# A two-layer decoder trunk: gates begun before the queries are done, one result slot, query groups moved in the order, and key weights with their own memory

## The chip, the cores and the metric

One core of one Trainium2 chip runs the whole program. The metric is the device time of one execution in microseconds (us), lower is better. TensorE (PE) multiplies matrices, VectorE (DVE) and ScalarE (ACT) do elementwise work, GpSimd (POOL) does powers and fills, SyncE (SP) issues the DMAs. PEld is PE's weight loader.

## What is computed

512 prompt tokens and 64 sample tokens (8 sequences of 8) pass through two layers. Cut to what matters:

```python
h = rmsnorm(x, g_norm)                                   # 1024 channels
rq, rk, rv, rz, aq, ak, av, az, iq, ik, iw, gr, ga = in_projection(h, w_in, ...)
o_r, s_new = retention(rq, rk, rv, ret_s0)               # 4 heads, state 128 x 128
u_r = (group_norm_heads(o_r) * silu(rz)) @ w_o_ret
# indexer: score = sum_h relu(iq_h . ik) * iw_h ; keep the top 128 (prompt) or 66 (sample) keys
o_a = softmax attention of aq over the kept keys          # 8 query heads, 2 key heads of 64
u_a = (o_a * silu(az)) @ w_o_att
m = sigmoid(gr) * u_r + sigmoid(ga) * u_a                 # the gates: 1024 channels each
x = x + m @ w_out
x = x + sigmoid(x @ w_ple_gate) * (p_i @ w_ple_proj)
```

Keys, values, indexer keys and retention states are outputs too.

## The kernel before

**Numbers and tiles.** All 576 tokens are handled together. A float32 product is made of three matmuls in a reduced-precision float32 form: each operand is split into a high part (`xh`, `whi`, by ACT) and a rest (`xl`, `wlo`, by DVE), and high x high, rest x high and high x rest are added up. Where channels are the rows of the result (`proj_a`: az, rq, rk, rz, gr, ga, wout, wpg), one unit gives 128 channels by 576 tokens in two halves of 288 columns, 24 matmuls each. Where tokens are the rows (`proj_b`: iq, rv, aq; `proj_kx`: the keys), a unit runs over five token tiles `j`, of which 0 to 3 are the prompt and 4 is the sample.

**The order.** The program is written as many generators ("streams"). A planner in the kernel (`Streams.go`, line 284) simulates the five engines with a table of durations (`_duration`) and emits next, of all streams' next instructions, the one that could start first; ties go to the smaller priority number. So it fixes each engine's order before anything runs. `Event` and `Slots` only steer the planner; on the chip the waits are semaphores. Priorities are in `PRIO`: 0 for the evacuations of projections and weight conversion, 3 for attention and the sample's indexer, 4 for sample retention, 5 for sample attention, 6 for prompt retention, 7 for the prompt's indexer with its top-k.

**The main stream** (priority 9) is the projections in the order of `PLAN`, one after another: kx, iq, rv0, rv1, az0 to az3, rt0, aq0, rt1, aq1, rt2, rt3 (rt is rq, rk and rz of a head), then the 16 gates gr and ga, then merge (wo), wout, pp, wpg. It writes into three PSUM banks "pm", and each half or tile is evacuated by a stream of its own.

**Weights** come by DMA into two staging tiles `WST` and are split into three pairs `WHI`, `WLO` by `convert`, which give their staging tile back. `drop` frees a pair after its unit.

**Side streams.** `indexer(j)` scores keys and finds the top-k on DVE. `attend` takes the query groups (j, u) in order: j = 0 to 3, u = 0, 1 (aq0 and aq1). Each is two `pair` streams that add into the one bank "oT", then `collect` multiplies the result, from POOL, into the tile `silz`. A query tile stays in one of four slots `QS` until its group is through. `attend_s` uses "oT" for the sample. `ret_p(h)` and `ret_s(h)` do the retention of head h, one head at a time; when both have used the head's rotated q and k, they set `e_hd[h]`. The buffers for q and k alternate between two heads, so `ropeT` of head 2 waits for `e_hd[0]` and of head 3 for `e_hd[1]`. The prompt state leaves through the small tiles `SO` and the store `out_rsp`.

**The gates** (line 1306) wait, before gr0, as follows, and then take one of four slots `ZS` in the tile `misc`, whose columns the query and indexer evacuations use before:

```python
if name == "gr" and i[0] == 0:
    for e in list(e_q.values()) + list(e_iq.values()) + [e_k, e_rr]:
        yield e
    ZS = zslots(0, 4)
z = yield Get(ZS)
```

A gate's two halves are multiplied with `R` (DVE, misc<-pm,R) and passed through tanh (ACT); `spill` then stores the gate to DRAM (`zgr`, `zga`), from where the merge fetches it. The merge starts when all side streams are done, by splitting `silz` into `oh` and `ol`.

**The start.** `load(k)` brings x by channel tile, and after x0 the norm gains `gn`, which the first split of x needs; `load_weights` brings the key weights in five parts (`KX_PARTS`) through `WST`. `setup2` brings the constants and the page table. `proj_kx` runs as x and weights arrive.

Of the kernel before, what the change touches and what calls it, by code (L numbers as in the profile page):

```python
# [11 lines left out]
FT = mybir.dt.float32  # L12
FR = mybir.dt.float32r
# [3 lines left out]
OP = mybir.AluOpType  # L17
# [88 lines left out]
class Op:  # L106
    __slots__ = ("eng", "fn", "a", "k", "name", "outs", "ins", "dur", "form", "banks")

    def __init__(self, eng, fn, name, a, k):
# [9 lines left out]
        if eng in ("DVE", "ACT") and len(self.ins) and self.outs[0][1] != self.ins[0][1]:  # L119
            self.dur += 0.12  # L120
# [25 lines left out]
def _duration(eng, name, out, aps, a, k):  # L146
# [21 lines left out]
    if eng == "POOL":  # L168
        return 0.3 + (0.165 if k.get("op", a[-1]) == OP.pow else 0.0022) * n
# [154 lines left out]
def tile_hybrid_decoder(ctx: ExitStack, tc: tile.TileContext, A, O):  # L324
# [51 lines left out]
    WST = slots(cp, "wst", [128, 1024], FT, 2)  # L376
    WHI = slots(cp, "whi", [128, 1024], FR, NSLOT["hi"])
    WLO = slots(cp, "wlo", [128, 1024], FR, NSLOT["lo"])
# [32 lines left out]
    second, third = Event(), Event()  # L411
# [4 lines left out]
    class Unit:  # L416
        def __init__(self, srcs):
            self.srcs, self.parts, self.ev = srcs, [], Event(len(srcs))
            self.evs = [Event() for _ in srcs]

    def plan(l):
# [7 lines left out]
        for st in PLAN:  # L429
# [3 lines left out]
            elif name == "iq":  # L433
                srcs = b(("wq",), 260, 3)
# [10 lines left out]
            u = Unit(srcs)  # L445
# [5 lines left out]
    def load_weights(units):  # L451
        for n, (u, src, size) in enumerate(units):
            if n == 1:
                yield second
            if n == 3:
                K.set(third)
            t = yield Get(WST)
            yield SP.dma_start(t[:, :size], src)
            K.spawn(convert(u, t, size, stage_ev[n], stage_ev[n + 1]), PRIO["convert"])

    def convert(u, t, size, prev, done):
        yield prev
        hi = yield Get(WHI)
        lo = yield Get(WLO)
        yield S.activation(hi[:, :size], t[:, :size], AF.Copy)
        yield V.tensor_tensor(lo[:, :size], t[:, :size], hi[:, :size].bitcast(FT), OP.subtract)
        K.put(WST, t)
# [52 lines left out]
    def proj_kx(u, xh, xl, evs):  # L520
# [3 lines left out]
        for i, (k0, k1) in enumerate(KX_PARTS):  # L524
# [16 lines left out]
            K.put(WHI, u.parts[i][0])  # L541
            K.put(WLO, u.parts[i][1])
# [17 lines left out]
    def put_x(x, k, l, xh, xl, zs, first):  # L560
        yield S.activation(xh[:, k, :T], x, AF.Copy, scale=gn[:, l, k:k + 1])
        yield V.scalar_tensor_tensor(xl[:, k, :], x, gn[:, l, k:k + 1], xh[:, k, :T].bitcast(FT),
                                     op0=OP.mult, op1=OP.subtract)
        yield S.activation(xh[:, k, T:TX], xl[:, k, NP:T].bitcast(FT), AF.Copy)
        if k == 0:
# [12 lines left out]
    def layer(l, xh, xl, kxb):  # L578
# [15 lines left out]
        e_r, e_rq, e_rr = Event(), Event(), Event()  # L594
# [45 lines left out]
        SO = slots(at, "so", [128, 128], FT, 2)  # L640
# [22 lines left out]
        def tables():  # L663
            yield e_rq
            yield SP.dma_start(rot, A["rot"])
            yield V.tensor_tensor(cosr, cosr, R, OP.mult)
# [170 lines left out]
        def indexer_s():  # L837
            yield paged
            kt = yield Get(S4)
            for b in range(8):  # L840
# [438 lines left out]
        la = None  # L1279
        for st in PLAN:  # L1280
# [4 lines left out]
            elif name == "iq":  # L1285
                yield from proj_b(U("iq"), 260, 3, xh, xl, (1, 4, 2, 3), iqx)
# [19 lines left out]
            elif name in ("gr", "ga"):  # L1306
                if name == "gr" and i[0] == 0:
                    for e in list(e_q.values()) + list(e_iq.values()) + [e_k, e_rr]:
                        yield e
                    ZS = zslots(0, 4)  # L1310
                z = yield Get(ZS)
                ev = Event(2)

                def gate(z, ev):
                    def evac(ps, cs):
                        yield V.tensor_tensor(z[:, cs], ps[:, :TH], R[:, cs], OP.mult)
                        K.put(BANK["pm"], ps)
                        yield S.activation(z[:, cs], z[:, cs], AF.Tanh, scale=0.5)
                        K.set(ev)
# [3 lines left out]
                def spill(z, ev, dst):  # L1323
                    yield ev
                    yield SP.dma_start(dst, z)
                    K.put(ZS, z)

                K.spawn(spill(z, ev, zd[(l,) + st]), 0)
                yield from proj_a(U(*st), 0, mv, KT, gate(z, ev))
# [68 lines left out]
        pst = lb.tile([128, 2, T], FT, name="pst")  # L1398

# [79 lines left out]
        def ple2(d, th, ev):  # L1479
# [3 lines left out]
            else:  # L1483
# [4 lines left out]
                yield from put_x(xa[:, d], d, l + 1, nh, nl, ZS, e_sq)  # L1488
                K.set(e_n[d])
                yield SP.dma_start(xd[:, d, :], xa[:, d])  # L1490
            K.set(e_e)
# [13 lines left out]
    def main():  # L1505
# [13 lines left out]
        def load(k):  # L1519
            x = st.tile([128, T], FT, name=f"x{k}")  # L1520
            if k > 3:
                yield third
            yield SP.dma_start(x, A["xT"][:, k, :])
            if k == 0:
                yield SP.dma_start(gn, A["norm_gain"])
                K.set(second)
            yield from put_x(x, k, 0, xh, xl, zs, e_sq)
            K.set(evs[k])

        for k in range(KT):  # L1530
            K.spawn(load(k), 2 if k else 0)
# [9 lines left out]

KX_PARTS = ((0, 1), (1, 2), (2, 4), (4, 6), (6, 8))
# [18 lines left out]
NSLOT = dict(s4=3, qs=4, t2=5, pt=1, hi=3, lo=3)  # L1561


def _prepare(x_prompt, x_sample, cache_k, cache_v, cache_idx_k, state_ret, page_table, p_prompt, p_sample,
# [13 lines left out]
    d["norm_gain"] = c(chan(norm_gain).transpose(2, 0, 1))  # L1578
    d["qk_gain"] = c(np.stack([np.asarray(q_norm_gain), np.asarray(k_norm_gain)], 1).reshape(-1))
    d["xT"] = c(chan(tok(x_prompt, x_sample)).transpose(2, 1, 0))  # L1580
# [63 lines left out]
```

## Time and profile before

| | us |
|---|---|
| median of 3 runs | 1098.57 |
| lowest, highest | 1097.22, 1099.5 |
| the profiled execution | 1100.1 |
| its span, first to last instruction | 1098.2 |
| PE busy | 1074.9 (98%) |
| DVE busy | 759.6 (69%) |
| ACT busy | 527.4 (48%) |

Busy PE is modelled, since matmuls are pipelined; the number of PE instructions in a stretch tells more than its busy time. Layer 0 runs from 0 to about 570 us and layer 1 from there to the end, with the same stages: keys, projections with attention and retention beside them (DVE nearly full), gates, merge, output projections. All instructions of the program are recorded at one line, so groups are told apart by the names of tiles: a matmul pm<-xh,whi is a `proj_a` unit, pm<-whi,xh a `proj_b` tile.

### The profile page before, as it was taken

What the parts mean: (1) busy time and instruction counts of PE and PEld (TensorE: products, weight loads), DVE (VectorE), ACT (ScalarE), POOL (GpSimd) and SP (SyncE); (2) the same over time, 40 slices, a digit from 0 to 9 for tenths busy, and PEclk for the clock granted to TensorE, in tenths of its full rate; (3) what the DMA queues carried; (4) which work ended last, traced back from release to release, by engine and by line L of the source; (5) the groups of instructions that cost most, each with busy time, mean ns of one, the idle gap of its engine ahead of it and who ended that gap; (6) DMA issues with size and microseconds to landing.
All of it is one profiled execution on the core that took longest, in us unless ns stands there. A gap on an engine that the chain in (4) does not pass through costs nothing.

```text
span 1098.2 us, 21521 instructions
## 1 busy us (share of the span) xinstructions
PE 1074.9 (98%) x8330; PEld 1048.6 (95%) x8330; DVE 759.6 (69%) x1963; ACT 527.4 (48%) x1112; POOL 68.6 (6%) x110
## 2 busy tenths in 40 slices
PE   7999999999999999999999999999999999999998
PEld 7989999989999999999999998999899999999998
DVE  6799999985455576543658999999854556655343
ACT  6743355676455442335446433656654555222421
POOL 0200012111000000000011001121101000000000
PEclk9999999999999999999999999999999999999999
DMA  6531222223333265533344322223232324554231
GB/s 204 162 118 69 88 80 96 76 83 110 113 103 108 103 198 158 184 93 104 99 124 133 108 71 74 81 99 106 91 121 91 121 90 144 184 184 136 82 115 49
DMA packets 53112, 124.85 MB, mean 114 GB/s; under 512 B 7443, under 2 KB 19603, under 8 KB 53011
## 3 DMA queue, kind: packets, MB, share of 16 engines
q1 hardware_dynamic: 53010, 123.49, 34.7%
q8 instruction: 65, 1.06, 0.4%
q14 instruction: 37, 0.30, 0.1%
HBM read 103.12 MB, written 20.35 MB: 112 GB/s over the span
## 4 chain that ended last, share of the span: by engine, by line
PE 68%; DVE 24%; issue 3%; DMA 1%; ACT 1%; SPq 1%; POOL 0%; DVEq 0%; POOLq 0%; ACTq 0%
PE pm L309 57%; DVE xl L309 6%; DVE sm L309 4%; DVE wlo L309 3%; PE tq L309 3%; PE oT L309 3%; DVE misc L309 2%; PE ta L309 2%; PE acc L309 2%; DVE silz L309 2%; PE tr L309 1%; DVE iqs L309 1%; DVE qs L309 1%; DVE tb L309 1%; DVE t2k L309 1%
## 5 line engine op out<-in xcount | busy, mean ns | idle before, releaser
L309 PE MATMUL pm<-xh,whi 128*128 128x288 f32 x1536 | 458.1, 298 | 0.0
L309 PE MATMUL pm<-xh,wlo 128*128 128x288 f32 x1536 | 457.5, 298 | 0.0
L309 PE MATMUL pm<-xl,whi 128*128 128x288 f32 x1536 | 457.2, 298 | 0.0
L309 PEld LDWEIGHTS pm<-xh,whi 128*128 128x128 f32 x1536 | 290.1, 189 | 1.2
L309 PEld LDWEIGHTS pm<-xl,whi 128*128 128x128 f32 x1536 | 290.2, 189 | 1.1 <-issue 0.2
L309 PEld LDWEIGHTS pm<-xh,wlo 128*128 128x128 f32 x1536 | 289.8, 189 | 0.9
L309 ACT ACTIVATE whi<-wst 128x1024 fp32r<-128x1024 f32 (+4 forms) x148 | 149.9, 1016 | 202.3 <-PE pm L309 135.0
L309 DVE TENSOR_TENSOR wlo<-wst,whi 128x1024 fp32r<-128x1024 f32 (+4 forms) x148 | 174.1, 1178 | 78.1 <-ACT whi L309 77.7
L309 PE MATMUL pm<-wlo,xh 128*128 128x256 f32 (+2 forms) x416 | 115.8, 287 | 1.7 <-DVE wlo L309 1.7
L309 PE MATMUL pm<-whi,xh 128*128 128x256 f32 (+2 forms) x416 | 117.0, 288 | 0.0
L309 PE MATMUL pm<-whi,xl 128*128 128x256 f32 (+2 forms) x320 | 91.6, 286 | 0.0
L309 ACT ACTIVATE t2k<-t2k,sm 128x256 f32<-128x256 f32 (+3 forms) x110 | 63.1, 579 | 43.7 <-DVE sm L309 42.2
L309 PEld LDWEIGHTS pm<-wlo,xh 128*128 128x128 f32 x416 | 78.7, 189 | 2.5 <-DVE wlo L309 2.3
L309 PEld LDWEIGHTS pm<-whi,xh 128*128 128x128 f32 x416 | 78.8, 189 | 1.9 <-issue 1.6
L309 PE MATMUL pm<-oh,whi 128*128 128x288 f32 x240 | 70.9, 296 | 0.0
L309 PE MATMUL pm<-oh,wlo 128*128 128x288 f32 x240 | 70.9, 295 | 0.0
L309 PE MATMUL pm<-ol,whi 128*128 128x288 f32 x240 | 70.8, 295 | 0.0
L309 PEld LDWEIGHTS pm<-whi,xl 128*128 128x128 f32 x320 | 60.5, 189 | 0.1
L309 DVE TENSOR_TENSOR misc<-pm,R 128x288 f32<-128x288 f32 x64 | 29.1, 455 | 42.1 <-PE pm L309 41.2
L309 DVE MAX8 sm<-xl 128x8 f32<-128x384 f32 (+2 forms) x96 | 52.2, 550 | 1.0
L309 DVE MATCH_REPLACE8 xl<-sm,xl 128x256 f32<-128x256 f32 (+2 forms) x96 | 51.7, 540 | 0.0
L309 DVE TENSOR_TENSOR ptl<-ta,pth 128x512 fp32r<-128x512 f32 (+1 forms) x48 | 28.6, 597 | 28.0 <-ACT pth L309 27.9
(261 smaller groups left out, 1723.7 us busy)
## 6 DMA issues: line engine op xcount, KB each, us to landing
wst<-in_wa SPq DMA_DIRECT2D x96, 512.0 KB, 3.5
wst<-in_wb SPq DMA_DIRECT2D x16, 512.0 KB, 4.0
wst<-in_wo SPq DMA_DIRECT2D x16, 512.0 KB, 3.9
zgr<-misc SPq DMA_DIRECT2D x16, 288.0 KB, 2.0
zga<-misc SPq DMA_DIRECT2D x16, 288.0 KB, 2.1
misc<-zgr SPq DMA_DIRECT2D x16, 288.0 KB, 2.8
misc<-zga SPq DMA_DIRECT2D x16, 288.0 KB, 4.6
s<-in_ckv SPq DMA_DIRECT2D x32, 128.0 KB, 2.4
```

Source lines behind the costliest of these rows:

```text
L309: op.fn(*op.a, **op.k)
```

## The change

- **Gates.** gr0 waits only for `e_k` (keys done) and `e_rq` (`R` done). There is one slot `ZS` at first; a stream `more` adds three when all queries and indexer tiles are done. The slot is now taken by the evacuation of a gate's first half, not ahead of its matmuls, and the second half's evacuation stores the gate itself.
- **Order.** aq0 goes ahead of az0, aq1 ahead of rt1.
- **Key weights.** The converted key weights of both layers have tiles of their own (`kxw`), and in layer 0 the raw ones too (`kxs`), so they take no `WST`, `WHI` or `WLO` (in layer 1 they still pass `WST`). In layer 0 their loads are issued at set places between those of x (`STEPS`), and the first conversion is on DVE.
- **Norm gains** come as 16 more columns of x0 (`x0`) and are copied to `gn` by POOL; the first split of x reads them from x0 itself. All x are issued by one stream, and the constants after them.
- **Buffers of 1040 columns** let iq's weights come in two parts of four channel tiles instead of three of up to three.
- **One `SO`** instead of two. The sample's gathers wait for the issue of the `rot` table. In the output stage the square of x comes after its split and its store.
- **The planner's table**: match_replace takes 60 columns more, a fill on POOL 0.32 us, an ACT instruction with up to 64 partitions 0.12 us more (instead of any with shifted partitions).

The diff, cut to its core:

```diff
-        if eng in ("DVE", "ACT") and len(self.ins) and self.outs[0][1] != self.ins[0][1]:
+        if eng == "DVE" and len(self.ins) and self.outs[0][1] != self.ins[0][1]:
+            self.dur += 0.12
+        if eng == "ACT" and self.outs[0][2] - self.outs[0][1] <= 64:
             self.dur += 0.12
...
+        if name == "match_replace":
+            return (n + 124) / 0.96e3
...
-    WST = slots(cp, "wst", [128, 1024], FT, 2)
+    WST = slots(cp, "wst", [128, 1040], FT, NSLOT["st"])
...
-                srcs = b(("wq",), 260, 3)
+                srcs = b(("wq",), 260, 4)
...
     def load_weights(units):
         for n, (u, src, size) in enumerate(units):
-            if n == 1:
-                yield second
-            if n == 3:
-                K.set(third)
-            t = yield Get(WST)
+            own = None
+            if u.kx is not None:
+                yield go_kx[n] if u.kx == 0 else e_kxw
+                a, z = (k * 320 for k in KX_PARTS[u.srcs.index((src, size))])
+                own = [w[:, a:z] for w in kxw[u.kx]]
+            if u.kx == 0:
+                t = kxw["raw"][:, a:z]
+            else:
+                t = yield Get(WST)
             yield SP.dma_start(t[:, :size], src)
...
+        if first:
+            yield V.tensor_copy(hi[:, :size], t[:, :size])
+        else:
+            yield S.activation(hi[:, :size], t[:, :size], AF.Copy)
...
-        SO = slots(at, "so", [128, 128], FT, 2)
+        SO = slots(at, "so", [128, 128], FT, 1)
...
             elif name in ("gr", "ga"):
-                if name == "gr" and i[0] == 0:
-                    for e in list(e_q.values()) + list(e_iq.values()) + [e_k, e_rr]:
-                        yield e
-                    ZS = zslots(0, 4)
-                z = yield Get(ZS)
-                ev = Event(2)
+                if ZS is None:
+                    yield e_k
+                    yield e_rq
+                    ZS = zslots(0, 1)
+
+                    def more():
+                        for e in list(e_q.values()) + list(e_iq.values()):
+                            yield e
+                        for z in zslots(1, 4).free:
+                            K.put(ZS, z)
+
+                    K.spawn(more(), 0)
...
+                        if cs.start == 0:
+                            z = yield Get(ZS)
...
+                        if cs.start:
+                            yield ev
+                            yield SP.dma_start(dst, z)
+                            K.put(ZS, z)
...
+        if l + 1 < DEPTH:
+            kxw[l + 1] = kx_tiles(lb, l + 1)
+            K.set(e_kxw)
...
+        def load():
+            for k in range(KT):
+                x = st.tile([128, T if k else T + DEPTH * KT], FT, name=f"x{k}")
+                yield SP.dma_start(x, A["xT"][:, k, :] if k else A["x0"])
+                K.spawn(take(k, x), 0)
+                if k in STEPS:
+                    K.set(go_kx[STEPS.index(k)])
+            K.set(third)
...
+STEPS = (0, 1, 3, 5, 7)
...
-PLAN = _plan("kx iq rv0 rv1 az0 az1 az2 az3 rt0 aq0 rt1 aq1 rt2 rt3")
+PLAN = _plan("kx iq rv0 rv1 aq0 az0 az1 az2 az3 rt0 aq1 rt1 rt2 rt3")
```

## Rows read from the trace of the kernel before

**Rows 1.** The page, busy time, share of the span and instructions of each engine.

```profile
PE 1074.9 (98%) x8330; PEld 1048.6 (95%) x8330; DVE 759.6 (69%) x1963; ACT 527.4 (48%) x1112; POOL 68.6 (6%) x110
```

**Rows 2.** Stretches: length, busy time (instructions) of each engine, clock, DMA share, GB/s.

```profile
120.00:238.00 118.00, 114.74 (x923) 110.76 (x922) 114.07 (x362) 66.10 (x157) 18.99 (x25) 1.00 0.26 87
238.00:250.00 12.00, 9.84 (x52) 8.07 (x51) 8.27 (x20) 7.59 (x20) 0.09 (x1) 0.72 0.24 87
250.00:262.00 12.00, 12.00 (x125) 11.04 (x124) 6.16 (x29) 6.53 (x17) 2.07 (x5) 1.00 0.16 51
400.00:560.00 160.00, 160.00 (x1203) 159.99 (x1202) 87.13 (x122) 61.37 (x99) 1.00 (x5) 1.00 0.41 129
...
783.00:793.00 10.00, 8.77 (x58) 7.34 (x59) 8.18 (x23) 5.96 (x16) 0.77 (x1) 1.00 0.32 113
```

**Rows 3.** Timeline, PE, layer 0: start, length, instruction, [idle before <- released by].

```profile
249.53 0.40 PE L309 MATMUL pm<-xh,whi 128*128 128x288 f32 x1
```

**Rows 4.** Timeline, DVE, layer 0: a query tile and a gate result.

```profile
250.83 0.43 DVE L309 TENSOR_TENSOR qs<-ta,qs 64x256 fp32r<-64x256 f32 x1
...
255.42 0.43 DVE L309 TENSOR_TENSOR misc<-pm,R 128x288 f32<-128x288 f32 x1
```

**Rows 5.** Timeline, PE, layer 1.

```profile
786.64 0.49 PE L309 MATMUL acc<-xh 128*128 128x128 f32 x2 [0.37 <-ACT xh L309]
...
790.88 0.38 PE L309 MATMUL pm<-xh,whi 128*128 128x288 f32 x1
```

**Rows 6.** Timeline, POOL: attention results of both layers.

```profile
375.89 0.74 POOL L309 TENSOR_TENSOR silz<-t2k,silz 128x256 f32<-128x256 f32 x1 [23.82 <-DVE t2k L309]
...
753.57 0.76 POOL L309 TENSOR_TENSOR silz<-t2k,silz 128x256 f32<-128x256 f32 x1 [2.35 <-DVE t2k L309]
...
774.91 0.72 POOL L309 TENSOR_TENSOR silz<-t2k,silz 128x256 f32<-128x256 f32 x1
...
924.39 0.74 POOL L309 TENSOR_TENSOR silz<-t2k,silz 128x256 f32<-128x256 f32 x1 [23.86 <-DVE t2k L309]
```

**Rows 7.** Timeline, DVE and ACT: aq1's first tile (layer 1), the merges' first splits.

```profile
384.92 1.24 ACT L309 ACTIVATE oh<-silz 128x576 fp32r<-128x576 f32 x2
...
724.54 0.43 DVE L309 TENSOR_TENSOR qs<-ta,qs 64x256 fp32r<-64x256 f32 x1
...
925.66 1.81 ACT L309 ACTIVATE oh<-silz 128x576 fp32r<-128x576 f32 x3
```

**Rows 8.** Timeline, ACT and PE, at both layers' start.

```profile
3.92 0.78 ACT L309 ACTIVATE xh<-x,gn 128x576 fp32r<-128x576 f32 x1 [1.68 <-DMA gn<-in_norm_gain]
...
5.10 0.64 PE L309 MATMUL oT<-whi,xh 128*128 128x320 f32 x1 [5.10 <-ACT whi L309]
...
12.48 0.41 PE L309 MATMUL oT<-wlo,xh 128*128 128x320 f32 x1 [0.47 <-DVE wlo L309]
...
39.93 0.39 PE L309 MATMUL pm<-wlo,xh 128*128 128x256 f32 x1 [0.79 <-DVE wlo L309]
...
583.02 0.39 PE L309 MATMUL pm<-wlo,xh 128*128 128x256 f32 x1 [0.44 <-DVE wlo L309]
```

**Rows 9.** Timeline, DVE and SP, layer 0: head 1's last gate half, its store, rt3's rotation.

```profile
169.98 0.46 DVE L309 TENSOR_TENSOR silz<-pm,R 128x288 f32<-128x288 f32 x1
...
213.75 0.42 SPq L309 DMA_DIRECT2D out_rsp<-so  x1
...
217.74 0.45 DVE L309 TENSOR_TENSOR xl<-pm,rot 128x288 f32<-128x288 f32 x1
```

**Rows 10.** Groups of instructions (busy us, mean ns) and DMA issues (KB, us to landing).

```profile
L309 DVE TENSOR_TENSOR misc<-pm,R 128x288 f32<-128x288 f32 x64 | 29.1, 455 | 42.1 <-PE pm L309 41.2 <-issue 0.3
...
L309 ACT ACTIVATE misc<-misc 128x288 f32<-128x288 f32 x64 | 27.9, 436 | 23.5 <-DVE misc L309 23.3
...
zgr<-misc SPq DMA_DIRECT2D x16, 288.0 KB, 2.0
...
out_rsp<-so SPq DMA_DIRECT2D x8, 64.0 KB, 3.1
```

More of the change, by code (lines that the diff above doesn't have):

```diff
@@ L410, in tile_hybrid_decoder, with __init__ @@
     ready, paged = Event(), Event()
-    second, third = Event(), Event()
+    third, e_kxw = Event(), Event()
+    kxw = {}
+    go_kx = [Event() for _ in KX_PARTS]
     W = {}
     class Unit:
-        def __init__(self, srcs):
-            self.srcs, self.parts, self.ev = srcs, [], Event(len(srcs))
+        def __init__(self, srcs, kx=None):
+            self.srcs, self.parts, self.ev, self.kx = srcs, [], Event(len(srcs)), kx
             self.evs = [Event() for _ in srcs]
@@ L452, in load_weights, with kx_tiles, convert @@
         for n, (u, src, size) in enumerate(units):
-            if n == 1:
-                yield second
-            if n == 3:
-                K.set(third)
-            t = yield Get(WST)
-            yield SP.dma_start(t[:, :size], src)
-            K.spawn(convert(u, t, size, stage_ev[n], stage_ev[n + 1]), PRIO["convert"])
-    def convert(u, t, size, prev, done):
-        yield prev
-        hi = yield Get(WHI)
-        lo = yield Get(WLO)
-        yield S.activation(hi[:, :size], t[:, :size], AF.Copy)
+            own = None
[7 more added lines that the diff above has]
+                t = yield Get(WST)
+            yield SP.dma_start(t[:, :size], src)
+            K.spawn(convert(u, t, size, stage_ev[n], stage_ev[n + 1], own, n == 0), PRIO["convert"])
+    kxs = None
+    def kx_tiles(pool, l):
+        return [pool.tile([128, KT * 320], FR, name=f"kx{i}{l}") for i in range(2)]
+    def convert(u, t, size, prev, done, own, first):
+        yield prev
+        if own is None:
+            hi = yield Get(WHI)
+            lo = yield Get(WLO)
+        else:
+            hi, lo = own
+        if first:
+            yield V.tensor_copy(hi[:, :size], t[:, :size])
+        else:
+            yield S.activation(hi[:, :size], t[:, :size], AF.Copy)
         yield V.tensor_tensor(lo[:, :size], t[:, :size], hi[:, :size].bitcast(FT), OP.subtract)
-        K.put(WST, t)
+        if u.kx != 0:
+            K.put(WST, t)
         K.set(u.evs[len(u.parts)])
@@ L558, in rsqrt, with put_x, square @@
         K.put(RSM, m)
[L560 to L563, printed above, removed]
+    def put_x(x, k, gain, xh, xl):
+        yield S.activation(xh[:, k, :T], x, AF.Copy, scale=gain)
+        yield V.scalar_tensor_tensor(xl[:, k, :], x, gain, xh[:, k, :T].bitcast(FT), op0=OP.mult, op1=OP.subtract)
         yield S.activation(xh[:, k, T:TX], xl[:, k, NP:T].bitcast(FT), AF.Copy)
+    def square(x, k, zs, first):
         if k == 0:
@@ L1278, in layer @@
         zt = {}
-        la = None
+        la = ZS = None
         for st in PLAN:
@@ L1517, in main, with take @@
         st = stc.__enter__()
[L1519 to L1523, printed above, removed]
+        def take(k, x):
+            gain = gn[:, 0, k:k + 1]
             if k == 0:
-                yield SP.dma_start(gn, A["norm_gain"])
-                K.set(second)
-            yield from put_x(x, k, 0, xh, xl, zs, e_sq)
+                yield G.tensor_copy(flat(gn), x[:, T:])
+                x, gain = x[:, :T], x[:, T:T + 1]
+            yield from put_x(x, k, gain, xh, xl)
             K.set(evs[k])
-        for k in range(KT):
-            K.spawn(load(k), 2 if k else 0)
+            yield from square(x, k, zs, e_sq)
+        def load():
[6 more added lines that the diff above has]
+            K.set(third)
+        kxw[0] = kx_tiles(st, 0)
+        kxw["raw"] = st.tile([128, KT * 320], FT, name="kxs")
+        K.spawn(load(), PRIO["load"])
         K.spawn(setup2(), 3)
```

41 lines of the change are left out of this document (23 added, 18 removed).

## The prediction

> **What bounds the kernel now.** I read the engine totals first: PE is busy 98% of the span, DVE 69% [rows 1]. So only time in which PE has too little to do can be won. Next comes the table of stretches, for instructions and not for busy time [rows 2]. In the dense tail of layer 0 PE issues 1203 instructions in 160 us, one per 0.133 us: that is its full pace. From 120 to 238 it keeps 923 in 118 us, a mix with short transposes, while DVE is busy 114 of 118 us: both are full. Then 238 to 250 holds only 52 instructions, at a mean granted clock of 0.72 (part of it at the lower of the two levels), and the next 12 us hold 125 at 1.00. In layer 1 the same place, 783 to 793, holds 58 in 10 us at 1.00.
>
> Third, the timeline there. In both layers PE has only side work (attention, retention) whose pieces wait for ACT or DVE, as at 786.64, until plain projections resume at 249.53 and 790.88 [rows 3, 5]. These are the first gate's. In the code, gr0 first waits for every query and indexer event. The last query tile is written on DVE at 250.83 in layer 0, and the first gate result at 255.42 [rows 4]. That tile is late because aq1 needs one of four "qs" slots, which come free only as attention finishes earlier pairs: the gates hang on attention.
>
> **The change, part by part.** All sums are against the profiled execution: span 1098.2, 1100.1 with what lies around it, 1.5 above the median of 1098.57.
>
> *Early gates.* gr0 now waits for e_k and e_rq alone, both set long before. The first gates fill the two holes.
> - Layer 0: 52 instructions at the pace of the next 12 us (12.00 / 125 = 0.096) need 5.0 us, at the full-column pace of 0.133 they need 6.9. Lost: 5.1 to 7.0 of 12. I take 6.0, as the hole's pieces are of the kinds around it, some longer.
> - Layer 1: 58 need 5.6 to 7.7 of 10; lost 2.3 to 4.4. I take 3.0, nearer the low end, since gate matmuls already fill the last 2 us [rows 5].
>
> The lowered clock is inside the layer-0 figure, not added to it.
>
> Here a rule decides how the hole is read. By PE's busy column the holes are 12 - 9.84 = 2.2 and 10 - 8.77 = 1.2 us, together 3.4; by the weight-load column 3.9 and 2.7 [rows 2]. The Trainium skill, Perfetto Trace Analysis, section "Identifying the Most-Contended Engine", says that matmul busy share is no good measure and that weight-load busy time is. The trace agrees: two neighbouring stretches of 82% and 100% busy differ by 52 against 125 instructions. By the page's measure the holes would be worth 6.6 instead of my 9.0 us, and the time 1092; by the busy column 1095. Both lie within the forecast's own range below.
>
> *One result slot.* A gate's slot is taken at its first half's evacuation. It holds half a gate (24 matmuls at 0.133 = 3.2), the second evacuation 0.455, tanh 0.436 and the store 2.0 to landing [rows 10]: 6.1 us against 6.4 of PE per gate. So one slot just keeps up, and three more come when all queries are done. Cost 0; up to 1 us for every us that DVE is late, for two or three gates.
>
> *Query groups ahead.* aq0 moves from behind rt0 to before az0, aq1 from behind rt1 to before it. This carries more than it seems. Attention runs pair after pair through one accumulator bank ("oT"); in layer 1 from the second group's first tile at 724.54 to the last result at 924.39, 200 us without a break, and the merge's first split starts at 925.66 [rows 6, 7]. Gates that end 3 us sooner would there just wait for attention. Layer 0 has slack: 375.89 and 384.92. With aq1 ahead of rt1 (three units of 6.4 us) that chain starts about 19 us earlier, more than the 3 needed. What hides the move: both groups do the same work, and their DVE work now falls before the light az units. What is late next is PE's own stream.
>
> *What the move brings closer.* rt2 and rt3 write the buffers of heads 0 and 1, so rt3's first rotary step on DVE waits until head 1's retention is through. In layer 0 head 1's last gate half comes at 169.98, its state is stored at 213.75 (43.8 us later), and rt3's first rotary step is at 217.74 (47.8 later) [rows 9]. Without aq1 in between (112 matmuls of 256 columns; at 256/288 of 0.133 each, 0.118, that is 13.2 us) that step wants to run 34.6 us after: 9.2 us too early. Queued behind it on DVE: the other rotary steps; behind those PE's three "pm" banks. Two more halves (6.4 us) fit in the banks, then PE stalls, 2.8 us. It shrinks where side work is ready, and DVE, relieved, serves head 1 sooner. Bounds per layer: 0 and 9.2. I take +2 for both layers together, as side work has filled most waits of this kind.
>
> *Start.* The gain weights come with x0, so the first ACT step no longer waits for a second load (it waited until 3.92), and the first weight conversion goes to DVE beside it instead of behind it; first matmul at 5.10 [rows 8]. Gain 0 to 0.9 (at most that step's 0.78, behind which the conversion stood, and a little of the wait); I take 0.4. The wait before 12.48 (0.47) came from a key-weight part that itself waited for a shared staging buffer; with own memory it goes: 0.5. The indexer weights in two parts instead of three and earlier value weights touch the stall before 39.93 (0.79): I take 0.5 of it. But constants and page table now queue on SP and the DMA engines behind two 520 KB loads: 0 to 1 us lost; I take 0, since their first use stands behind the key matmuls.
>
> *Layer 1 key weights in own memory.* Their five parts stop taking conversion buffers at the end of layer 0, so the value weights convert sooner: the wait before 583.02 is 0.44 [rows 8]. I take 0.4; the key matmuls themselves had no gap.
>
> *No gain by themselves:* one "so" buffer instead of two (a store lands in 3.1 us [rows 10], and the users come far further apart); 1040 columns (the same bytes); the second copy of the gain on POOL, idle there. The planner's new durations only reorder; I value them at 0, with 3 us on either side, since they move every instruction's place a little.
>
> Sum: -6.0 - 3.0 - 0.4 - 0.5 - 0.5 - 0.4 + 2.0 = -8.8. From the profiled 1100.1 that is 1091.3; from the median of 1098.57 it is 1089.8. I say **1090**.
>
> **Rivals.**
> 1. *The other small stalls go too.* With gates to draw on and durations nearer the truth, PE also fills waits elsewhere: between 120 and 238 PE idles 3.3 us and its weight loader 7.2 [rows 2], and about as much in layer 1. Half of 14: 1083. Against it: the gates still stand behind rt3 in the order, so they can't fill what comes before.
> 2. *Attention still ends last in layer 1.* If DVE, full until 238, gives the earlier queries no earlier service, the chain keeps its 924 and layer 1's 3 us are not won: 1093. Against: evacuations of projections are served first on DVE, top-k last, so top-k gives way.
> 3. *The change doesn't do what it says.* The main stream is in order; if it reaches gr0 no sooner relative to attention, or waits at rt3 instead, the hole only moves: 1098.
> 4. *Slower: head 1 holds rt3.* Attention goes before retention on DVE (priority 3 against 6), and its pairs for the second block now come before head 1 is through. One such step took 774.91 - 753.57 = 21 us in layer 1 [rows 6]. If half of that, 10 us, lands on head 1, rt3 wants its buffer 19 us too early, less 6.4 in the banks: 13 us of stall in each layer instead of 1, or +24: 1114. The break-even is 5.5 us of stall per layer, a delay of 3 to 4 us. For it: DVE has 4 us to spare in 118 there. Against it: while rt3 waits, DVE has no new evacuations and turns to head 1.
>
> **How the numbers follow.** Forecast 0.52, its own range 1084 to 1096 (the holes' bounds, the 3 us of reordering and the stall's 0 to 5). Rival 1 has 0.13, rival 2 0.10, rival 3 0.10, rival 4 0.15, spread from 1101 to 1115. Within 0.2% (2.2 us, about what a measurement of this kernel can tell from no change) lies rival 3 alone: faster 0.75, same 0.10, slower 0.15. The range is 1081 to 1102: it takes in the first four cases but the far end of rival 1, and the near end of rival 4; about 0.17 is left out.
>
> **What would show it.** Early gates right: no stretch of 10 us near the end of rt3 with under 70 PE instructions, granted clock 1.00 throughout; first gate result before the last query tile. Queries ahead right: last attention result in layer 1 at least 10 us before the merge's first split. Start right: first matmul near 4.7, no wait near 12. Rival 4: PE waits on a rotary result or on "pm" just before rt3's head, and a state store within 4 us before it. The prediction is wrong if the holes are gone and the span is not at least 5 us shorter: then the time came back as stalls between rt0 and rt3.

## The result and the profile after

The changed kernel takes 1081.42 us (1081.24 to 1081.85) against 1097.89 for the kernel before on the same chip: a ratio of 0.9848 (0.9832 to 0.9864). It is faster, as forecast, but by 16.5 us where 8 to 9 were forecast. The time lies at the low edge of the stated range, and below the forecast's own range of 1084 to 1096. The profiled spans are 1080.1 and 1098.2, so 18.1 us have to be found.

The page's engine totals and granted clock (compare [rows 1]):

```profile
PE 1066.7 (99%) x8330; PEld 1045.4 (97%) x8330; DVE 758.4 (70%) x1962; ACT 526.5 (49%) x1109; POOL 70.9 (7%) x111
...
PEclk9999999999999999999999999999999999999999
```

PE does the same 8330 instructions; nothing was taken away from it. So the 18.1 us are time in which PE waited, or worked more slowly at the lower clock; both are called idle here. Stretches of the kernel after: from the end of rv1 to the end of rt3 in each layer, and the first 12 and 10 us of gates (length, then busy time and instructions of PE, PEld, DVE, ACT, POOL; clock; DMA share; GB/s):

```profile
71.23:234.16 162.93, 161.09 (x1259) 155.80 (x1257) 159.91 (x481) 87.37 (x197) 20.48 (x26) 1.00 0.26 86
605.83:767.50 161.67, 159.44 (x1249) 155.09 (x1248) 159.66 (x480) 86.54 (x198) 17.07 (x26) 1.00 0.26 86
...
234.00:246.00 12.00, 12.00 (x129) 10.68 (x131) 8.35 (x28) 6.95 (x17) 1.80 (x3) 1.00 0.16 45
...
767.00:777.00 10.00, 10.00 (x106) 9.04 (x106) 6.38 (x23) 6.18 (x14) 1.66 (x3) 1.00 0.23 82
```

The two holes of [rows 2] are gone: where 52 and 58 instructions stood, 129 and 106 stand, at clock 1.00. The same stretches from rv1 to rt3 in the kernel before:

```profile
74.87:238.38 163.51, 159.93 (x1254) 155.30 (x1254) 159.38 (x487) 84.09 (x190) 18.99 (x25) 1.00 0.26 86
617.70:782.69 164.99, 161.10 (x1257) 155.78 (x1256) 160.03 (x487) 83.82 (x191) 18.44 (x24) 1.00 0.25 85
```

Timeline, PE, after: first key matmul, first gate matmuls, and the longest wait of PE near rt3's start in layer 1 (start, length, instruction, [idle before <- released by]); compare [rows 3, 5, 8]:

```profile
4.65 0.61 PE L315 MATMUL oT<-kx,xh 128*128 128x320 f32 x1 [4.65 <-ACT xh L315]
...
234.29 0.29 PE L315 MATMUL pm<-xh,whi 128*128 128x288 f32 x1
...
756.14 0.38 PE L315 MATMUL oT<-ptl,vhl 128*128 128x256 f32 x1 [1.34 <-DVE ptl L315]
...
767.63 0.30 PE L315 MATMUL pm<-xh,whi 128*128 128x288 f32 x1
```

Timeline, DVE and SP, after, in order of time in each layer: head 1's state store and rt3's first rotary step, the last query tile, the first gate result; compare [rows 4, 9]:

```profile
219.87 0.34 SPq L315 DMA_DIRECT2D out_rsp<-so  x1
...
222.84 0.45 DVE L315 TENSOR_TENSOR xl<-pm,rot 128x288 f32<-128x288 f32 x1
...
226.10 0.43 DVE L315 TENSOR_TENSOR qs<-ta,qs 64x256 fp32r<-64x256 f32 x1
...
238.71 0.45 DVE L315 TENSOR_TENSOR misc<-pm,R 128x288 f32<-128x288 f32 x1
...
759.71 0.43 DVE L315 TENSOR_TENSOR qs<-ta,qs 64x256 fp32r<-64x256 f32 x1
...
775.43 0.45 DVE L315 TENSOR_TENSOR misc<-pm,R 128x288 f32<-128x288 f32 x1
```

The last query tile now comes 8 us *before* rt3's end in both layers (226.10 against 234.3, 759.71 against 767.6). The last attention result of layer 1 and the merge's first split there (POOL, ACT; compare [rows 6, 7]):

```profile
893.98 0.74 POOL L315 TENSOR_TENSOR silz<-t2k,silz 128x256 f32<-128x256 f32 x1 [23.85 <-DVE t2k L315]
...
908.02 2.40 ACT L315 ACTIVATE oh<-silz 128x576 fp32r<-128x576 f32 x4
```

**Where the time went.** Busy time stretches when PE waits, so idle is counted from instructions: the length of a stretch less the sum, over its PE instructions, of the usual step from one of that shape to the next (the median step in the kernel before, 0.133 us for 288 columns; for four short shapes, which mostly wait, a low step). By this count PE's work is 1050.5 us in every run here. Other steps for the short shapes move a stretch's idle by up to a us or more, but its change from run to run by about half a us.

| stretch (idle of PE, us) | before | after | change | forecast |
|---|---|---|---|---|
| start of layer 0 to the end of rv1 | 12.5 | 9.6 | -2.9 | -1.4 |
| layer 0, rv1 to rt3's end | 7.8 | 6.3 | -1.5 | +1 |
| layer 0, first four gates (the hole) | 7.2 | 1.8 | -5.4 | -6.0 |
| layer 1, iq, rv0, rv1 | 2.1 | 0.7 | -1.5 | -0.4 |
| layer 1, rv1 to rt3's end | 9.2 | 5.9 | -3.3 | +1 |
| layer 1, first four gates (the hole) | 3.9 | 1.5 | -2.4 | -3.0 |
| all other | 4.9 | 3.8 | -1.1 | 0 |
| sum | 47.7 | 29.6 | -18.1 | -8.8 |

The holes came out as forecast (-7.8 for -9.0). The surprise is the two stretches up to rt3, 4.8 us better instead of 2 worse, and more at both layers' starts (-4.4 for -1.8). Their causes took experiments.

### The profile page after: what moved, and what is told of

The parts are those of the page before. It is cut to its first block, busy times and chain, and to the rows that moved or that the text cites. A ratio compares the mean times of both kernels' runs of the same rounds, so it can differ in the third digit from the quotient of the medians.

```text
span 1080.1 us, 21464 instructions
## 1 busy us (share of the span) xinstructions
PE 1066.7 (99%) x8330; PEld 1045.4 (97%) x8330; DVE 758.4 (70%) x1962; ACT 526.5 (49%) x1109; POOL 70.9 (7%) x111
## 4 chain that ended last, share of the span: by engine, by line
PE 72%; DVE 22%; issue 2%; ACT 1%; DMA 0%; POOL 0%; SPq 0%; DVEq 0%; ACTq 0%; POOLq 0%
PE pm L315 60%; DVE xl L315 5%; DVE sm L315 4%; PE tq L315 3%; DVE wlo L315 3%; PE oT L315 3%; PE acc L315 2%; DVE misc L315 2%; PE ta L315 2%; PE tr L315 2%; DVE silz L315 2%; DVE t2k L315 1%; DVE qs L315 1%; DVE sc L315 1%; DVE iqs L315 1%
## 5 line engine op out<-in xcount | busy, mean ns | idle before, releaser
L315 ACT ACTIVATE whi<-wst 128x1024 fp32r<-128x1024 f32 (+1 forms) x136 | 143.8, 1057 | 192.0 <-PE pm L315 123.3
L315 DVE TENSOR_TENSOR wlo<-wst,whi 128x1024 fp32r<-128x1024 f32 (+1 forms) x136 | 166.9, 1227 | 66.4 <-ACT whi L315 66.2
L315 PE MATMUL pm<-wlo,xh 128*128 128x256 f32 (+1 forms) x384 | 106.4, 285 | 0.2 <-DVE wlo L315 0.2
L315 PE MATMUL pm<-whi,xh 128*128 128x256 f32 (+1 forms) x384 | 106.1, 284 | 0.0
L315 ACT ACTIVATE t2k<-t2k,sm 128x256 f32<-128x256 f32 (+3 forms) x118 | 66.8, 573 | 52.4 <-DVE sm L315 48.4
L315 PE MATMUL pm<-whi,xl 128*128 128x256 f32 (+1 forms) x304 | 86.1, 283 | 0.0
L315 PEld LDWEIGHTS pm<-wlo,xh 128*128 128x128 f32 x384 | 72.3, 188 | 1.5 <-issue 0.8
L315 PEld LDWEIGHTS pm<-whi,xh 128*128 128x128 f32 x384 | 72.4, 188 | 1.0 <-issue 0.8
L315 PEld LDWEIGHTS pm<-whi,xl 128*128 128x128 f32 x304 | 57.2, 188 | 0.1
L315 DVE MAX8 sm<-xl 128x8 f32<-128x512 f32 (+2 forms) x96 | 52.3, 552 | 0.8
```

Source lines behind the costliest of these rows:

```text
L315: op.fn(*op.a, **op.k)
```

## The experiments

Theory at first: early gates fill the holes, the order keeps attention from ending last, the planner's durations only reorder. Rivals: one part does it all; or the durations do what lies outside the holes. The change has four separable parts, so each was undone by itself, and then made by itself.

**Each part undone.** Edits to the kernel after:

```diff
@@ no_early_gates
...
+                if name == "gr" and i[0] == 0:
+                    for e in list(e_q.values()) + list(e_iq.values()) + [e_k, e_rr]:
+                        yield e
+                    ZS = zslots(0, 4)
+                z = yield Get(ZS)
...
@@ old_order
-PLAN = _plan("kx iq rv0 rv1 aq0 az0 az1 az2 az3 rt0 aq1 rt1 rt2 rt3")
+PLAN = _plan("kx iq rv0 rv1 az0 az1 az2 az3 rt0 aq0 rt1 aq1 rt2 rt3")
@@ old_durations
-        if name == "match_replace":
-            return (n + 124) / 0.96e3
...
@@ old_memory
...
+    WST = slots(cp, "wst", [128, 1024], FT, 2)
...
```

(old_durations takes back all three lines of the table; old_memory takes back the key weights' own memory, the packed gains, the loading order, the 1040 columns and the late square.)

> The changed kernel, but gr0 waits again for every query, indexer, key and rotary event and gates take one of four slots ahead of their matmuls. Theory A (the gates fill the holes): PE's holes before the first gate come back, some 8 us of idle (5.4 in layer 0, 2.4 in layer 1), 1089. Rival B (the earlier query groups alone would have closed the holes, because the last query tile now comes at 226 us and rt3 ends at 234): no hole, within 2 us of the changed kernel, 1081 to 1083.

> The changed kernel with the old order az0 to az3, rt0, aq0, rt1, aq1, rt2, rt3. Theory A (early gates fill holes, but in layer 1 the attention chain then binds the merge): layer 0 keeps its time, layer 1 loses its 2.4 us of hole, and the stretch from aq0 to rt3 gets its old idle time back (1.5 us in layer 0, 3.3 in layer 1), so about 1088. Rival B (the order made both the holes and the stalls go): 1093 or more. Rival C (the planner's durations closed the stalls): 1081 to 1084.

> The changed kernel with the planner's old table of durations (match_replace, POOL fills and ACT's narrow instructions as before). Theory C (durations nearer the truth closed the small stalls between the value weights and rt3): 4 to 6 us of PE idle return in those two stretches, 1086. Rival A (the query order closed them): within 2 us of the changed kernel.

> The changed kernel with the start and the key weights as before (shared staging and conversion buffers, gains loaded by themselves, iq in three parts, constants ahead of the last loads). Theory M (own memory gave the 3.6 us up to the end of rv1 in layer 0 and 1.8 us in layer 1): those waits return and the time is 1086 to 1087. Rival (those stalls were the plan's order, not the buffers): under 2 us lost.

| undone | us | ratio to before | what came back (idle of PE) |
|---|---|---|---|
| early gates | 1081.61 | 0.9840 (0.9824 to 0.9857) | nothing |
| order | 1086.38 | 0.9883 (0.9867 to 0.9900) | 5.4 at layer 1's merge |
| durations | 1091.33 | 0.9927 (0.9911 to 0.9944) | 4.9 and 4.6 from rv1 to rt3 |
| memory | 1087.15 | 0.9890 (0.9874 to 0.9907) | 2.8 from the start to rv1, 1.2 in layer 1's rv, the rest spread |

Two of my terms fall here. Without the early gates nothing is lost: under the new order the last query tile is there before gr0 asks for it (225.63 us, where rt3's last matmul starts at 233.68). And the durations, which I valued at 0, carry 9.9 us, 9.5 of it before rt3's end; I had expected 4 to 6. With the old order the early gates do close the holes, but attention then ends last in layer 1, as the forecast said it would. The 1.5 and 3.3 us that I expected back up to rt3 did not come. PE and POOL at that merge (old order):

```profile
912.12 0.40 PE L315 MATMUL pm<-oh,whi 128*128 128x288 f32 x1 [2.49 <-ACT oh L315]
...
912.38 1.30 POOL L315 TENSOR_TENSOR silz<-xl,silz 128x256 f32<-128x256 f32 x1 [23.86 <-DVE xl L315]
```

For the memory, the waits of the value weights' low parts, iq to rv1 of layer 0 (groups: count | busy, mean ns | idle before), first the old memory, then after:

```profile
L315 PE MATMUL pm<-wlo,xh 128*128 128x256 f32 (+1 forms) x82 | 22.8, 285 | 1.5 <-DVE wlo L315 1.5
```

```profile
L315 PE MATMUL pm<-wlo,xh 128*128 128x256 f32 (+1 forms) x81 | 22.3, 283 | 0.2 <-DVE wlo L315 0.2
```

**Each part alone**, the same edits made in the kernel before (memory_alone has the single `SO` and the wait for `rot` as well):

> The kernel before with the early gates and one result slot alone. Theory A': the hole in layer 0 is filled (5.4 us), but in layer 1 attention still ends at its old place and the merge waits for it, so layer 1 wins at most 1 us: 1092 to 1093 against 1098. Rival (holes in both layers are filled and attention follows): 1090. Rival (the gates alone do nothing, as in the changed kernel): 1097 to 1099.

> The kernel before with the new order of the query groups alone; gates wait as before for all query events. Theory A'': the order alone closes both holes (5.4 and 2.4 us), because the last query tile comes before rt3 ends; the small stalls up to rt3 stay, since the planner's durations are the old ones: 1089 to 1091. Rival: with the old durations the earlier groups cost stalls between rt0 and rt3, 1094 or more.

> The kernel before with the planner's new durations alone. Theory C: the stalls from the query groups to rt3 shrink (7.8 and 9.2 us of idle before, 6.3 and 5.9 in the changed kernel), the holes stay: 1092 to 1094. Rival (the durations pay only together with the new order): 1096 to 1099.

> The kernel before with the new start and the key weights' own memory (and with it one store tile, the 1040 columns, the packed gains and the awaited rotary load), old gates, order and durations. Theory M: 0.9 us to the end of iq, 2.0 to the end of rv1 and 1.5 in layer 1 are won, the rest keeps its place: 1093 to 1095. Rival (the buffers pay only with the new order): under 2 us.

| alone | us | ratio to before | idle up to rt3 (L0, L1) | holes (L0, L1) | at the merges |
|---|---|---|---|---|---|
| before | 1098.5 | 1 | 7.8, 9.2 | 7.2, 3.9 | -0.3, 4.4 |
| gates | 1102.26 | 1.0033 (1.0021 to 1.0046) | 7.8, 9.3 | 0.8, 1.2 | 5.9, 9.7 |
| order | 1094.13 | 0.9958 (0.9942 to 0.9975) | 8.9, 10.5 | 1.7, 1.4 | -0.3, 4.3 |
| durations | 1111.99 | 1.0130 (1.0108 to 1.0151) | 5.6, 5.1 | 14.4, 14.7 | -0.3, 4.3 |
| memory | 1107.56 | 1.0079 (1.0062 to 1.0096) | 8.8, 8.4 | 12.7, 12.8 | -0.4, 4.0 |

(The last column runs from gate 16 to the next layer's keys or to the end.) Alone the parts cost 3.8 - 4.4 + 13.5 + 9.1 = +22 us; together they gain 16.5. Gates, durations and memory took longer than any range I had given for them, and order fell in its rival's range, not in mine: the holes closed as I said, but idle up to rt3 rose by 1.1 and 1.3 us. In order alone the last query tile comes 10 and 18 us before rt3's last matmul starts (241.38, 783.49), where it came 12 and 10 us behind it before:

```profile
231.39 0.42 DVE L309 TENSOR_TENSOR qs<-ta,qs 64x256 fp32r<-64x256 f32 x1
...
765.91 0.43 DVE L309 TENSOR_TENSOR qs<-ta,qs 64x256 fp32r<-64x256 f32 x1
```

Gates alone show the second half of the forecast's mechanism at its purest: the holes shrink by 9.1 us, and 11.5 us come back as waits for attention at the two merges. Gates alone, PE and POOL at layer 1's merge:

```profile
927.71 0.40 PE L309 MATMUL pm<-oh,whi 128*128 128x288 f32 x1 [2.50 <-ACT oh L309]
...
927.98 1.30 POOL L309 TENSOR_TENSOR silz<-t2k,silz 128x256 f32<-128x256 f32 x1 [23.93 <-DVE t2k L309]
```

**Why durations alone double the holes and more.** The traces gave a new theory. In the planner the bank oT goes to whoever asked first. With durations alone the sample's attention gets it ahead of the query group (1,1), that is j = 1, u = 1, on whose query slot the last query tile waits. Durations alone: ACT reads the sample's result (so<-oT) and then the group's (t2k<-oT); DVE writes the last query tile:

```profile
250.43 0.28 ACT L315 ACTIVATE so<-oT 128x128 f32<-128x128 f32 x1 [1.16 <-PE oT L315]
...
261.69 0.38 ACT L315 ACTIVATE t2k<-oT 64x256 f32<-64x256 f32 x1 [1.93 <-PE oT L315]
...
263.74 0.43 DVE L315 TENSOR_TENSOR qs<-ta,qs 64x256 fp32r<-64x256 f32 x1
```

The test asks the planner for the other turn and for nothing else; `e_two` is set when the group (1,1) holds oT (edit to durations alone):

```diff
@@ durations_sample_behind
...
                 yield e_sc[4]
+                yield e_two
...
```

> The kernel before with the new durations alone (which took 1112.0), and in it the sample's attention asks for the oT bank only once the attention pair (1,1) holds it. Theory C: the holes of 14.4 and 14.7 us of durations alone are there because the sample's attention, some 15 us of oT, slips in ahead of (1,1), on whose slot the last query tile waits (263.7 and 811.3 us; 31.7 us from the third result to the fourth instead of 17). Behind it the holes are at most 7 and 4 us as in the kernel before, and the waits up to rt3 stay at 5.6 and 5.1: 1088 to 1096. Rival D: the pair is late because its own scores come late on DVE; then moving the sample leaves the holes above 11 us each: 1105 to 1112.

It took 1096.69 (0.9976; 0.9966 to 0.9986), 15 us less. Memory alone shows the same turn, though nobody reversed it there: ACT reads the sample's result at 246.60 and that of (1,1) at 258.58. Its single `so` tile adds to it, since that read waits for an earlier store to leave:

```profile
246.60 0.28 ACT L309 ACTIVATE so<-oT 128x128 f32<-128x128 f32 x1 [2.67 <-DMA out_rsp<-so]
...
258.58 0.38 ACT L309 ACTIVATE t2k<-oT 64x256 f32<-64x256 f32 x1 [2.54 <-PE oT L309]
```

In layer 1 that wait is 2.69 us. So one `so` buffer, which the forecast put at no cost, holds up oT there; in the kernel after nothing waits for such a store. In the test on durations alone the turn is reversed and the last query tile 13 us earlier:

```profile
246.46 0.77 ACT L315 ACTIVATE xl<-oT 64x256 f32<-64x256 f32 x2 [0.59 <-PE oT L315]
...
269.60 0.28 ACT L315 ACTIVATE so<-oT 128x128 f32<-128x128 f32 x1 [1.98 <-PE oT L315]
...
250.29 0.43 DVE L315 TENSOR_TENSOR qs<-ta,qs 64x256 fp32r<-64x256 f32 x1
```

The holes fall from 14.4 and 14.7 to 9.2 and 5.1 us. Theory C holds for most of it, rival D falls. My figures of 7 and 4 were low, and the time 0.7 us above my range: the group's result is read hardly earlier than in the kernel before (246.46 against 248.17 us), while rt3 ends 2.3 and 4.8 us earlier, and that stands as hole.

**Do early gates ever count?** Edits: gates and durations together in the kernel before; and early gates undone where the price of match_replace is old and the last query tile comes 4 us behind rt3's end.

> The kernel before with two parts: early gates with one slot, and the new durations (gates alone 1102.3, durations alone 1112.0). Theory E (early gates fill whatever hole the late query tile leaves, and give it back only as far as attention then ends last): the holes of 14.4 and 14.7 us fall to about 2 each, 25 us less; attention (last results 376.8 and 921.8 in durations alone) then ends after the gates, as in gates alone, and costs 5 to 8 us at each merge: 1096 to 1102. Rival F (parts add up): 1112.0 + 1102.3 - 1098.5 = 1116.

> The kernel after with the old price of match_replace (1090.4) and without early gates. There the last query tile came at 245.1 and 784.4, behind the end of rt3 (about 240.6 and 780.9), and PE still idled only 2.2 and 1.7 us. Theory E: the early gates covered this; without them idle of 2 to 5 us per layer comes back: 1093 to 1098, while without them the kernel after itself lost nothing. Rival G (early gates are worth nothing in any case under the new order): 1090 to 1091.

Gates and durations took 1098.98 (1.0007; 0.9998 to 1.0017), not the 1116 of added parts, so there E holds: the holes fall to 1.9 and 3.1 us, and the merges wait 5.1 and 9.5. There the gates are worth 13 us. But 1090.44 (0.9928; 0.9911 to 0.9944) without them at the old price equals 1090.38 with them, so G holds there and E does not: a tile 4 us late costs nothing measurable. PE does not wait for that tile itself. The plan only puts 18 and 9 instructions of side work ahead of the first gate matmul, which starts at 242.68, before the tile at 244.16. Early gates are an insurance against a query tile that is late by much more than that (26.6 us in layer 0 of durations alone).

**What in the durations counts.** Edits to the kernel after, in the line `return (n + 124) / 0.96e3` of match_replace: 64 (which is the old rule), 124 with the rest of the table old, 154, 184, 264; last, 184 for match_replace and for max.

> The kernel after, with the old table but for match_replace, which keeps its 60 columns more. Theory A (the top-k's price is what counts): the old table takes each of the 57 match_replace of a layer 62 ns too short, 3.6 us of DVE per layer that the plan did not see, just where DVE is full. With the new price alone the waits up to rt3's end stay near 6 us in each layer: 1081 to 1084. Rival B (any change of the table only shuffles the order): no link with this line, the time falls anywhere from 1081 to 1091, the value with the old table whole.

> The kernel after, where only match_replace has its old price, and the other two lines of the table are new. Theory A: as with the whole old table, 1089 to 1092, with about 11 and 10 us of PE waits up to rt3's end instead of 6.3 and 5.9. Rival B: anywhere from 1081 to 1091; if both this one and the one with the new price alone lie below 1084, the table's lines replace one another.

> The kernel after, with match_replace priced at 90 columns more instead of 60 (31 ns further up, about 10 ns per instruction above what was measured). Theory A: a price a little too high costs little, 1080 to 1085. Rival B: another shuffle, 1081 to 1091, as far from the kernel after as the old price is.

> The kernel after, with match_replace priced at 120 columns more than the old rule instead of 60 (at 90 it took 1079.4, at 60 1081.5, at 0 1090.4). Theory A (a true price is what helps, a little slack costs little): no more gain, 1079 to 1084, with about 5 to 6 us of PE waits up to rt3's end in each layer. Rival H (the higher the price the better, as top-k simply yields to the rest): a further 2 us, 1075 to 1078.

> The kernel after, match_replace priced at 200 columns more than the old rule, 208 ns (at 0, 60, 90, 120: 1090.4, 1081.5, 1079.4, 1077.4 us). Theory A (a truer plan helps, with a little slack): the plan now thinks DVE fuller than it is by some 8 us per layer, so work stands later in DVE's order than it could; the waits up to rt3 grow again or the last query tile comes late: 1080 to 1090. Rival H (top-k that yields helps, however far): 1073 to 1077.

> The kernel after, with match_replace and max both priced at 120 columns more than the old rule (match_replace alone: 1077.4). The old price of max is already about right: its steps of 0.60 us at 512 columns are 576 / 960. Theory A: a false price on a true one brings nothing more and may shuffle back: 1078 to 1086. Rival H: the added 125 ns on 57 max in each layer let top-k yield further: 1072 to 1077.

| columns added to n | us | ratio to before | idle up to rt3 (L0, L1) |
|---|---|---|---|
| 64 (rest new) | 1090.38 | 0.9919 (0.9902 to 0.9936) | 9.6, 11.6 |
| 124 (rest old) | 1082.46 | 0.9848 (0.9832 to 0.9865) | 6.7, 6.4 |
| 124, the kernel after | 1081.42 | 0.9848 (0.9832 to 0.9864) | 6.3, 5.9 |
| 154 | 1079.35 | 0.9819 (0.9803 to 0.9835) | 5.0, 4.8 |
| 184 | 1077.43 | 0.9811 (0.9794 to 0.9827) | 5.2, 3.3 |
| 264 | 1072.65 | 0.9761 (0.9744 to 0.9777) | 1.7, 1.0 |
| 184, and max too | 1074.31 | 0.9777 (0.9761 to 0.9794) | 1.9, 1.8 |

It is match_replace and hardly anything else of the table: with it alone the time is 1.0 us above the kernel after, at the same ratio to before. From 64 to 264 the idle falls by 18.5 us and the time by 17.7. But theory A, a *truer* price, does not reach that far. One match_replace of 512 columns steps to the next DVE instruction in 0.59 us, or in up to 0.71 where a max of its result comes next, and its value load adds 0.07: 0.66 to 0.78 in all.

```profile
236.06 0.09 DVE L315 MATCH_VALUE_LOAD xl<-sm,xl 128x8 f32 x1
236.13 0.68 DVE L315 MATCH_REPLACE8 xl<-sm,xl 128x512 f32<-128x512 f32 x1
236.73 1.22 DVE L315 TENSOR_TENSOR wlo<-wst,whi 128x1024 fp32r<-128x1024 f32 x1
```

The price is 0.66 at 124 and 0.81 at 264, above all of these, and it still helped, as did a price of 0.73 on a max whose step is 0.60. Rival H stands: a dearer top-k yields. Stretch rv1 to rt3 in both layers, at 64 and then at 264 columns:

```profile
70.97:240.57 169.60, 166.46 (x1331) 158.98 (x1329) 163.56 (x497) 88.86 (x205) 18.55 (x28) 1.00 0.28 89
608.95:780.95 172.00, 168.12 (x1331) 159.93 (x1330) 164.68 (x496) 89.72 (x206) 20.21 (x29) 1.00 0.27 87
```

```profile
71.45:231.01 159.56, 159.56 (x1284) 156.70 (x1281) 155.97 (x473) 87.51 (x200) 21.02 (x28) 1.00 0.27 88
600.81:757.59 156.78, 156.78 (x1249) 154.60 (x1247) 153.12 (x462) 86.10 (x196) 19.49 (x26) 1.00 0.27 89
```

At 264 PE is busy for all of both stretches, and DVE works 7.6 and 11.6 us less in them. That work stands later: the last match_replace of layer 0, at 64, 124 and 264 columns (rt3's last matmul starts at 240.6, 234.2 and 231.0):

```profile
219.05 0.68 DVE L313 MATCH_REPLACE8 xl<-sm,xl 128x512 f32<-128x512 f32 x1
```

```profile
236.13 0.68 DVE L315 MATCH_REPLACE8 xl<-sm,xl 128x512 f32<-128x512 f32 x1
```

```profile
244.13 0.67 DVE L315 MATCH_REPLACE8 xl<-sm,xl 128x512 f32<-128x512 f32 x1
```

Top-k leaves the stretch where DVE is full and goes into the gates, where it has room.

**Would the price alone have done it?** Edit to the kernel before: match_replace at n + 264.

> The kernel before with one line more: match_replace priced at 200 columns more in the planner's table. Theory I (the price shortens the waits up to rt3, but without the new order the last query tile still stands behind pair (1,1), so what is won there returns in the holes): waits up to rt3 fall from 7.8 and 9.2 us to 2 to 4 in each layer, the holes of 7.2 and 3.9 grow to 10 to 16: 1094 to 1112. Rival J (the price is worth as much by itself as in the kernel after, where it took 1090.4 to 1072.7): the holes stay at most as they were: 1080 to 1088.

No: 1110.55 (1.0103; 1.0087 to 1.0120). Theory I holds. Each layer from rv1 to rt3, and then to its first gate:

```profile
75.87:232.33 156.46, 156.46 (x1249) 153.34 (x1245) 151.88 (x457) 80.14 (x180) 18.04 (x24) 1.00 0.27 89
232.33:266.20 33.87, 24.50 (x170) 18.40 (x168) 23.75 (x80) 16.01 (x43) 3.44 (x8) 0.75 0.26 80
625.14:781.72 156.58, 155.74 (x1226) 151.92 (x1222) 150.63 (x454) 79.86 (x181) 19.33 (x25) 1.00 0.27 89
781.72:805.65 23.93, 17.10 (x147) 13.23 (x146) 21.25 (x70) 13.07 (x36) 2.18 (x5) 0.92 0.36 113
```

PE is nearly as dense up to rt3 as in the fastest kernel, and then spends 34 and 24 us until the first gate at some two fifths of its pace: idle 2.2 and 3.8, then 20.5 and 14.8 (in layer 0 more than I expected; the sample is read ahead of the group (1,1) here too, 251.79 against 263.82). The new order looks like what lets the price pay, since with it the last query tile comes before rt3's end (217.05 against 231.01 at 264 columns). That is argued: no run has the price and the new order without the other parts.

So the fastest kernel of the study is the kernel after with match_replace at n + 264: 1072.65 us, 8.8 below the kernel after.

## Why the prediction was right and wrong

- **What bounds it** was right: PE's idle is all that could be won, and the holes held what the instruction count said. By PE's busy share they were worth 3.4 us, by the measure of the Trainium skill (Perfetto Trace Analysis, "Identifying the Most-Contended Engine") 6.6, by my count 9.0; they gave 7.8. The trace agrees with the Trainium skill that busy share misleads, and the gain lies between its measure and my count.
- **Early gates, -9.0**: the size right, the owner wrong. The holes closed through the order. My own sign, "first gate result before the last query tile", shows it: 238.71 comes after 226.10. I took the move of aq0 and aq1 only for the end of attention, and did not follow it to the last query tile. The order alone moves that tile from 250.8 to 231.4 and from 793.1 to 765.9 us. That the sum had this term nearly right is luck: it was earned by another part.
- **Attention ends last in layer 1** without the order: right, and dearer than the 3 us of rival 2: 5.4 us with the old order, and both merges in gates alone. With it attention is done 13 us ahead (894.7 against 908.0), as forecast.
- **The durations at 0** is the step that failed. Between the end of rv1 and the end of rt3 they give 4.9 + 4.6 us. The bound of 3 us on either side had no row behind it. There was something to go by in the trace before: match_replace is 57 times in a layer, in layer 0 48 of them between rv1's and rt3's ends, where DVE is busy 159.4 of 163.5 us. Its new price, 62.5 ns more each, shifts 3.0 us there. Nearly all of the loss hangs on this one line: with it alone at its old price the kernel after takes 1090.38, and with the whole table old 1091.33. Rival 1 ("durations nearer the truth", 1083, chance 0.13) is what happened in size, and in half of its cause: the durations filled those waits, the gates did not. I set it low because the gates can't fill what lies before them, which is true of gates and says nothing of durations; and "truth" is not the whole reason, since a price above every measured step helped further.
- **rt3 behind head 1, +2**: the order of things was right, the price wrong. rt3's first rotary step does stand right behind head 1's store (219.87, then 222.84), but PE had no wait near it in layer 0, and in layer 1 the longest one in that place is 1.34 us, on an attention product. The side work that I counted on for part of the cover covered it all; rival 4 did not happen.
- **Start, -1.4, and layer 1's keys, -0.4**: the first matmul came 0.45 us earlier, as forecast (0.4), but the last key matmul of layer 0 started 0.07 us later (24.57, 24.64): the gain was lost again as idle between them (3.2 before, 3.7 after). The wait near 12 us shrank from 0.47 to 0.16 and was not gone. What was won lies further on. The indexer's stretch lost 0.9 us of idle and the value projections' 2.0 in layer 0 and 1.5 in layer 1, as buffers come free sooner. I had priced one wait of each kind where the projections have many. Mis-sized by 2.6 us (-4.4 for -1.8); the mechanism stands in the run with the old memory, where 2.8 and 1.2 us come back in these places.
- **Parts added up.** My sum took them as independent, but for one interaction. Made one by one they lose 22 us, undone one by one they lose 20.8, and together they gain 16.5.

Not settled: why the planner puts a dearer top-k behind the other work. Its rule takes the instruction that could start first, with the priority only for ties, so a priority of 7 holds top-k back little and a long price more; that is argued from the code. A long price also makes all of DVE look later to the plan, and no run parts this from top-k yielding. And where the price turns to a loss was not reached.

## What to carry to other kernels

Where a kernel's order comes from a table of durations, the price of work off the path is a lever of its own: try it several times over, and read its effect as the idle of the bounding engine per stretch. Before adding up the parts of a change, find the one event that each hole hangs on (here the last query tile, behind one bank's queue) and ask of every part whether it moves that event or the moment when it is needed. A part that loses by itself may be half the gain in company, so undo each one from the whole as well as making it alone.

## What the runs showed of the hardware

- PE's busy time fell by 8.2 us (1074.9 to 1066.7) with the same 8330 instructions, while the span fell by 18.1: matmuls that wait, or run at the lower clock, are recorded as longer, so nearly half of the idle was booked as work.
- The granted clock can fall in a hole: 0.75 and 0.92 in the waits of the price alone, 0.72 in layer 0's hole of the kernel before, 1.00 there in the kernel after. In the stretches under 1.00 PE ran partly at the lower of its two levels. It need not fall: in layer 1's hole of the kernel before, with 58 instructions in 10 us, it stayed at 1.00 [rows 2].
